# Splitting half of the down-projection weights by transfers instead of by ScalarE and VectorE

## The chip, the cores and the metric

The kernel runs on one core of one Trainium2 chip. The metric is the device time of one execution in microseconds (us). The kernel before takes 1150.3 us (median of two runs, 1150.1 and 1150.5).

## The reference

One layer of a hybrid model on 256 tokens of width 2048, all in float32: a normalized input is projected (`w_in`, 2048 x 6676), goes through three branches (an mLSTM, a forgetting attention, a conformer convolution), and is projected back (`w_out`). Then comes the feed-forward layer, in which the change lies:

```
x  = x + concat([y_m, y_a, y_c]) @ w_out
h2 = rmsnorm(x, norm_ffn)
x  = x + square(relu(h2 @ w_up)) @ w_down      # w_up 2048 x 8192, w_down 8192 x 2048
return rmsnorm(x, final_norm)
```

## The kernel before

**Products in parts.** Every float32 operand of a large product is held as two tiles in TensorE's float32r type: a high part (the value rounded) and a low part (value minus high part). A product is then three terms: high x high, high x low, low x high. `matmuls` (L397) issues them: for a block of kind A (`w_out`, `w_down`, some of `w_in`) three matmuls of 512 columns for each 128 rows of weights and each half of the tokens; for kind B (`w_up`, the rest of `w_in`) two matmuls for each 128 output columns, one of 512 and one of 256 columns.

**Weights.** They are streamed in units of one MiB (`unit`, L308: for 512 columns, four chunks of 128 rows). `load` (L328) brings a unit into one of `NRAW` = 4 `raw` tiles by one transfer from SyncE's queue. A unit is used in two halves. `split_tasks` (L357) makes the two parts of half `i`: ScalarE copies the half of `raw` into a tile `hi` (L368, the rounding), and VectorE writes `lo` = `raw` - `hi` (L387). There are `NHL` = 5 tiles each of `hi` and `lo`, so the parts of half `i + 5` can be made as soon as the matmuls of half `i` have read theirs. The load of unit `u + 4` is asked for when both halves of unit `u` are split (L395).

**Order.** The order of every engine's instructions is fixed when the program is built, by a list schedule: each `Task` has an engine, a cost in estimated us, dependencies and a priority; `best` (L146) takes the task that can start first by the estimated clocks of the engines, and `issue` (L133) emits it. A task is ready 0.15 (`LAT`) after a dependency on another engine ends. The main loop (L1208) walks the halves in order: it forces what half `i` needs, emits its matmuls, puts TensorE's clock forward by 2.6, and creates the split of half `i + 5` with that end as its dependency. The estimates set only the order; on the chip each instruction waits for its semaphores, and each engine (SyncE's and GpSimd's queues too) goes through its list in order.

**Feed-forward stage.** It runs by quarters of the hidden features (L1114): four up blocks of kind B, then four down blocks of kind A. A down block has 4 units, 8 halves, 96 matmuls. There are 64 units of `w_down`, so 64 even and 64 odd halves. The very last four halves are used twice, first by the upper 128 token rows, then by the lower (L1199). GpSimd has nothing to do in this stage; at the end it computes two small powers (`rsqrt`, L293) for the final norm.

Of the kernel before, what the change touches and what calls it, by code (L numbers as in the profile page):

```python
# [6 lines left out]
F32 = mybir.dt.float32  # L7
# [6 lines left out]
P = 128  # L14
# [19 lines left out]
def trunk(ctx: ExitStack, tc, x, norm_mix, w_in, b_in, mlstm_conv_w, mlstm_conv_b,  # L34
# [13 lines left out]
    def sbt(pl, shape, name, dt=F32, bufs=1, tag=None):  # L48
        return pl.tile(shape, dt, name=name, tag=tag or name, bufs=bufs)
# [8 lines left out]

    # ---- emission: a list schedule on estimated engine clocks
    clock = dict(act=0.0, dve=0.0, pool=0.0, pe=0.0, ctl=0.0)  # L60
# [5 lines left out]
    class Buf:  # L66
        """One tile of a rotation of n: taken when the tile n before it has no readers left."""
        def __init__(self, rot):
            self.rot, self.readers, self.t = rot, [], None
# [5 lines left out]
    class Task:  # L75
        def __init__(self, eng, cost, fn, deps=(), prio=10, table=None, takes=(), uses=()):
            self.eng, self.cost, self.fn, self.prio, self.table = eng, cost, fn, prio, table
            self.deps = [d for d in deps if d is not None]
            self.takes, self.fin = takes, None
            for b in uses:  # L80
                b.readers.append(self)
# [26 lines left out]
    def room(takes):  # L108
        """When the buffers are free; None while a reader of the old tile is not yet issued."""
        r = 0.0  # L110
        for b in takes:
            h = b.rot.hist
            if len(h) >= b.rot.n:
                for u in h[len(h) - b.rot.n].readers:
                    if u.fin is None:
                        return None
                    r = max(r, u.fin + LAT)
        return r
# [14 lines left out]
    def issue(t, r):  # L133
        e = t.eng
        queue[e].remove(t)
        take(t.takes)
        cost = t.cost
        if t.table and t.table != table[0]:
            cost += TABLE
            table[0] = t.table  # L140
        t.fn()
        t.fin = max(clock[e], r) + cost
        if e != "ctl":
            clock[e] = t.fin

    def best(e):  # L146
# [26 lines left out]
    def extras():  # L173
        """TensorE tasks whose operands are there by now."""
        while True:
            run(clock["pe"])
            p = best("pe")
            if not p or p[2] > clock["pe"] - MARGIN:
                return
            issue(p[1], p[2])  # L180
# [12 lines left out]

    # ---- pools
    pools = {}
# [19 lines left out]

    # ---- loads of x, parameter rows
    RAWN = 8 * 272
# [31 lines left out]

    # x lies where the values and the attention operands come later  # L250
    xt = [sbt(pl("mix"), [P, 2 * NH * (HD + 1)], "x0", tag="vaug")[:, 0:D], sbt(pl("mix"), [P, D], "x1", tag="fqk")]
# [4 lines left out]

    # ---- constants
    ident = sbt(base, [P, P], "ident")
# [29 lines left out]
    def small(n=2):  # L288
        """Columns of the tile of statistics."""
        nst[0] += n  # L290
        return st[:, nst[0] - n:nst[0]]
# [3 lines left out]

    # ---- weight stream
    units = []
# [10 lines left out]
    def unit(b, src, c0, k0, last, gates=0, gside=None):  # L308
        """One MiB of weights: columns c0.. of src (and the gate columns beside them)."""
        n = 4 if b.w == 512 else 8  # L310
        units.append(dict(b=b, src=src, c0=c0, ks=list(range(k0, k0 + n)), w=b.w,
                          g=gates, gside=gside, last=last, first=not b.started))
        b.started = True
# [14 lines left out]
    def load(u, now=0.0):  # L328
        if u >= len(units):
            return  # L330
        dma[0] = max(dma[0], now + 1.8) + 2.95
        loaded.setdefault(u, Task("none", 0.0, None)).fin = dma[0]
        d = units[u]
        t = raw_tile()
        n = len(d["ks"])
        w = d["w"] + d["g"]
        off = d["g"] if d["gside"] == "left" else 0
        c0 = d["c0"] - off
        vw = t[:, 0:n * w].rearrange("p (c w) -> p c w", c=n)
        k0 = d["ks"][0]  # L340
        parts = 2 if u == 0 else 1
        for i in range(parts):
            m = n // parts
            nc.sync.dma_start(vw[:, i * m:(i + 1) * m, :],
                              d["src"][(k0 + i * m) * P:(k0 + (i + 1) * m) * P, c0:c0 + w].rearrange(
                                  "(c p) w -> p c w", p=P))
        raws[u] = (vw[:, :, off:off + d["w"]], vw)
        if u == NRAW - 1:
            load_vb(C_V)
        if u == NRAW + 1:  # L350
            late_loads()
            params_in.fin = dma[0] + 6.0
# [4 lines left out]
    def split_tasks(i, deps):  # L357
        """High and low parts of half a unit."""
        u, h = divmod(i, 2)
        if u >= len(units):  # L360
            return
        d = units[u]
        n = len(d["ks"]) // 2

        def hi():
# [64 lines left out]
    big_tile("y")  # L430
    chunk = {}   # tasks that make chunk k of a stationary or moving operand

    # rows of the transposed products, halves summed: out = s * (ps_a + ps_b) + bias
    def join(o, b, i, bias=None, s=1.0, prio=0, deps=(), takes=()):
# [19 lines left out]

    # ---- parameter columns
    def cols_task(name, r0, r1, deps, prio=-3):
# [9 lines left out]

    # the array's clock rises once it is kept busy: transposes of the identity while x arrives
    def warm_up():
# [7 lines left out]

    # ---- x: norm, transpose, split
    xs_stat = [small(4) for _ in range(2)]
# [59 lines left out]

    # ---- late constants and parameters
    vb = {}  # L540
# [55 lines left out]

    # ---- values
    def blk(*a, **kw):
# [25 lines left out]

    # ---- conformer branch
    u_rot, g_rot = Rot(1), Rot(1)
# [99 lines left out]

    # ---- the other values, forgetting attention's operands
    b = block_units(blk("A", 512, xs, "x"), w_in, C_V + 512)
# [15 lines left out]

    # ---- gates
    gps, gsum, gtp = mx_buf(), mx_buf(), mx_buf()
# [13 lines left out]
    def build_gates():  # L760
# [11 lines left out]
        a_l = t_act(c1, lambda: act.activation(gl, gu, AF.Ln), [d_u], prio=3, table="ln")  # L772
        # log1p(e) = ln(u) + (e - (u - 1)) / u with u = fl(1 + e)
        d = t_dve(0.45, lambda: dve.scalar_tensor_tensor(ge, gu, -1.0, ge, op0=OP.add, op1=OP.subtract), [d_u], prio=3)
# [38 lines left out]

    # ---- heads, both kinds
    pw_rot, pt_rot, hh_rot = Rot(2), Rot(2), Rot(2)

    def head_out(num, nb, r, r_task, num_task, prio, put):
        """Root mean square norm of r * num by rows, transposed; put() takes the columns."""
        sq, t, sc = small(), small(), small()

        def f1():
            for j in range(2):
                act.activation(junk[:, 0:HD], num(j), AF.Square, accum_out=sq[:, j:j + 1])

        def f2():
            dve.tensor_mul(t, sq, r)
            dve.scalar_tensor_tensor(t, t, 1.0 / HD, r, op0=OP.mult, op1=OP.mult)
            dve.tensor_scalar(t, t, EPS, None, op0=OP.add)

        a = t_act(0.7, f1, [num_task], prio=prio, uses=[nb])  # L830
        d = t_dve(0.5, f2, [a, r_task], prio=prio)
        d = t_pool(0.5, lambda: rsqrt(t, t), [d], prio=prio)
        d = t_dve(0.15, lambda: dve.tensor_mul(sc, t, r), [d], prio=prio)
        hb, tb = Buf(hh_rot), mx_buf()

        def f3():
            hb.t = sbt(pl("mix"), [P, 2, HD], "hh", bufs=2)
            for j in range(2):
                act.activation(hb.t[:, j, :], num(j), AF.Copy, scale=sc[:, j:j + 1])

        a = t_act(0.6, f3, [d], prio=prio, takes=[hb], uses=[nb])

        def f4():
            tb.t = bank("mx")
            for j in range(2):
                pe.transpose(tb.t[:, j * P:(j + 1) * P], hb.t[:, j, :], ident)  # L846

        p = t_pe(0.25, f4, [a], prio=prio, takes=[tb], uses=[hb])
        return put(tb, p)

    # ---- forgetting attention
    def fox(h, prio):
# [4 lines left out]
        def scores():  # L857
            q, k = hold["fqk"][:, h // 2, h % 2, :], hold["fqk"][:, 2 + h // 2, h % 2, :]
            ps = sb.t = bank("mx")
            # F[l] is constant along a row and leaves its softmax as it is: -F[s] and the mask are added  # L860
            mul(ps[:, 0:384], sel[:, NH + h:NH + h + 1].to_broadcast([P, P]), em, True, False)
# [42 lines left out]

    # ---- mLSTM
    xpad = [None, None]
# [124 lines left out]

    # ---- after the mixer
    ob = [blk("A", 512, ys, "y") for _ in range(4)]
# [66 lines left out]

    # ---- feed-forward layer, by quarters of the hidden features
    z_rot, zz_rot = Rot(2), Rot(2)
# [92 lines left out]

    # ---- issue
    NU = len(units)
# [79 lines left out]
```

## Time and profile before

| | |
|---|---|
| time, median of 2 | 1150.3 us |
| span of the profiled execution | 1148.2 us (2.1 us below the median; its own time is not listed apart) |
| TensorE busy | 1133.9 us (99%) |
| VectorE busy | 717.3 us (62%) |
| ScalarE busy | 574.3 us (50%) |
| GpSimd busy | 17.6 us (2%) |
| granted TensorE clock, mean | 0.996 |
| transfers | 214.91 MB, mean 187 GB/s |

The span goes from the first to the last instruction. PE is TensorE, DVE VectorE, ACT ScalarE, POOL GpSimd, SP SyncE; "PE mm" and "PE mx" are matmuls into the two groups of PSUM banks. An arrow `<-` in a wait names what ended it. L387 is line 387 of the kernel.

### The profile page before, as it was taken

What the parts mean: (1) busy time and instruction counts of PE and PEld (TensorE: products, weight loads), DVE (VectorE), ACT (ScalarE), POOL (GpSimd) and SP (SyncE); (2) the same over time, 40 slices, a digit from 0 to 9 for tenths busy, and PEclk for the clock granted to TensorE, in tenths of its full rate; (3) what the DMA queues carried; (4) which work ended last, traced back from release to release, by engine and by line L of the source; (5) the groups of instructions that cost most, each with busy time, mean ns of one, the idle gap of its engine ahead of it and who ended that gap; (6) DMA issues with size and microseconds to landing.
All of it is one profiled execution on the core that took longest, in us unless ns stands there. A gap on an engine that the chain in (4) does not pass through costs nothing.

```text
span 1148.2 us, 14812 instructions
## 1 busy us (share of the span) xinstructions
PE 1133.9 (99%) x5880; PEld 965.3 (84%) x5880; DVE 717.3 (62%) x978; ACT 574.3 (50%) x807; POOL 17.6 (2%) x40
## 2 busy tenths in 40 slices
PE   8999999999999999999999999999999999999996
PEld 7888888888888888888888888888888888888885
DVE  6679988886665556556545655544655554566553
ACT  6455366777864545444344444333544333454442
POOL 1000000000000000000000000000000000000000
PEclk9999999999999999999999999999999999999999
DMA  8756654557546556655566655566655566655542
GB/s 304 242 184 191 199 164 148 151 153 248 169 162 220 184 185 184 190 199 196 184 189 193 189 193 190 184 191 195 189 193 187 184 192 199 190 189 184 183 147 74
DMA packets 127692, 214.91 MB, mean 187 GB/s; under 512 B 3676, under 2 KB 44936, under 8 KB 127240
## 3 DMA queue, kind: packets, MB, share of 16 engines
q1 hardware_dynamic: 127016, 212.92, 57.9%
q8 instruction: 46, 0.75, 0.3%
q10 hardware_dynamic: 608, 1.06, 0.3%
q14 instruction: 22, 0.18, 0.0%
HBM read 211.87 MB, written 2.10 MB: 186 GB/s over the span
## 4 chain that ended last, share of the span: by engine, by line
PE 97%; DMA 1%; issue 0%; ACT 0%; DVE 0%; SPq 0%; POOL 0%; POOLq 0%; ACTq 0%; DVEq 0%
PE mm L57 64%; PE mx L57 32%; DMA x<-in_x_dram 1%; PE mx L1085 0%; SPq L255 0%; PE mx L846 0%; POOL st L294 0%; PE mx L531 0%; ACT x2t L1188 0%; PE mx L879 0%; DVE lo L387 0%; ACT junk L1175 0%; POOLq L1272 0%; ACT hi L368 0%; PE mx L705 0%
## 5 line engine op out<-in xcount | busy, mean ns | idle before, releaser
L387 DVE TENSOR_TENSOR lo<-raw,hi 128x1024 fp32r<-128x1024 f32 x392 | 480.1, 1225 | 384.8 <-ACT hi L368 383.4
L368 ACT ACTIVATE hi<-raw 128x1024 fp32r<-128x1024 f32 x392 | 415.5, 1061 | 507.4 <-PE mm L57 317.8
L57 PE MATMUL mm<-x,hi 128*128 128x512 f32 x640 | 227.8, 400 | 0.0
L57 PE MATMUL mm<-h,hi 128*128 128x512 f32 x512 | 180.7, 397 | 0.0
L57 PE MATMUL mx<-h,hi 128*128 128x512 f32 x512 | 180.4, 397 | 0.0
L57 PE MATMUL mm<-x,lo 128*128 128x256 f32 x640 | 179.4, 280 | 0.0
L57 PE MATMUL mm<-hi,hid 128*128 128x512 f32 x512 | 159.0, 389 | 0.0
L57 PE MATMUL mx<-hi,hid 128*128 128x512 f32 x512 | 158.9, 389 | 0.0
L57 PEld LDWEIGHTS mm<-x,hi 128*128 128x128 f32 x640 | 120.2, 188 | 28.9 <-ACT tmp L443 0.4
L57 PE MATMUL mm<-h,lo 128*128 128x256 f32 x512 | 143.7, 281 | 0.0
L57 PE MATMUL mx<-h,lo 128*128 128x256 f32 x512 | 143.7, 281 | 0.0
L57 PEld LDWEIGHTS mm<-x,lo 128*128 128x128 f32 x640 | 120.9, 189 | 0.1
L57 PEld LDWEIGHTS mm<-h,hi 128*128 128x128 f32 x512 | 96.1, 188 | 23.3 <-DVE x2t L1073 0.2
L57 PEld LDWEIGHTS mx<-h,hi 128*128 128x128 f32 x512 | 96.1, 188 | 23.3
L57 PEld LDWEIGHTS mm<-hi,hid 128*128 128x128 f32 x512 | 96.1, 188 | 20.1
L57 PEld LDWEIGHTS mx<-hi,hid 128*128 128x128 f32 x512 | 96.1, 188 | 20.0
L57 PE MATMUL mm<-lo,hid 128*128 128x512 f32 x256 | 99.6, 389 | 0.0
L57 PE MATMUL mx<-lo,hid 128*128 128x512 f32 x256 | 99.6, 389 | 0.0
L57 PEld LDWEIGHTS mm<-h,lo 128*128 128x128 f32 x512 | 96.7, 189 | 0.2
L57 PEld LDWEIGHTS mx<-h,lo 128*128 128x128 f32 x512 | 96.7, 189 | 0.0
L57 PE MATMUL mm<-hi,y 128*128 128x512 f32 x256 | 80.4, 392 | 0.0
L57 PE MATMUL mm<-hi,x 128*128 128x512 f32 x192 | 61.6, 396 | 0.0
(191 smaller groups left out, 872.6 us busy)
## 6 DMA issues: line engine op xcount, KB each, us to landing
raw<-in_w_up_dram SPq DMA_DIRECT2D x64, 1024.0 KB, 5.3
raw<-in_w_down_dram SPq DMA_DIRECT2D x64, 1024.0 KB, 5.2
raw<-in_w_in_dram SPq DMA_DIRECT2D x45, 1024.0 KB, 5.3
raw<-in_w_out_dram SPq DMA_DIRECT2D x16, 1024.0 KB, 5.3
raw<-in_w_in_dram SPq DMA_DIRECT2D x4, 1032.0 KB, 5.1
raw<-in_w_in_dram SPq DMA_DIRECT2D x2, 1088.0 KB
x<-in_x_dram SPq DMA_DIRECT2D x8, 256.0 KB, 6.0
x2t<-in_x_dram SPq DMA_DIRECT2D x2, 1024.0 KB
```

The source lines that it names most:

```text
L57: pe.matmul(o, l, r, start=start, stop=stop, skip_group_check=True)
L368: act.activation(t, raws[u][0][:, h * n:(h + 1) * n, :], AF.Copy)
L387: dve.tensor_sub(hl[i][1], raws[u][0][:, h * n:(h + 1) * n, :], hl[i][0].bitcast(F32))
```

## The change

In the down projection the odd half of each unit is no longer loaded into `raw`. Two transfers from GpSimd's queue read it from memory instead: the first casts it to float32r into `hi`; ScalarE then writes the negated `hi` into `lo`; the second transfer reads the same weights again and adds them into `lo`. The even halves are split as before. The load of `w_down` brings the even half alone (512 KB), and the load of unit `u + 4` waits for the even half of unit `u` only. The planner's tasks get a `lag` that is added to a task's end but not to its engine's clock.

```diff
 class Task:
-    def __init__(self, eng, cost, fn, deps=(), prio=10, table=None, takes=(), uses=()):
+    def __init__(self, eng, cost, fn, deps=(), prio=10, table=None, takes=(), uses=(), lag=0.0):
...
+            self.lag = lag
...
 def issue(t, r):
         if e != "ctl":
             clock[e] = t.fin
+        t.fin += t.lag
...
 def load(u, now=0.0):
         parts = 2 if u == 0 else 1
+        if d["src"] is w_down:
+            n = n // 2
...
 def split_tasks(i, deps):
         n = len(d["ks"]) // 2
+        if h == 1 and d["src"] is w_down:
+            k1 = d["ks"][n]
+            src = w_down[k1 * P:(k1 + n) * P, d["c0"]:d["c0"] + d["w"]].rearrange("(c p) w -> p c w", p=P)
+
+            def f1():
+                t = sbt(base, [P, n, d["w"]], "hi", F32R, bufs=NHL)
+                hl[i] = [t, sbt(base, [P, n, d["w"]], "lo", F32R, bufs=NHL)]
+                pool_e.dma_start(t, src)
+
+            def f2():
+                act.activation(hl[i][1], hl[i][0].bitcast(F32), AF.Copy, scale=-1.0)
+
+            a = t_pool(1.0, f1, deps, prio=-1, lag=3.0)
+            a = t_act(ca(1024), f2, [a], prio=-1)
+            b = t_pool(1.0, lambda: pool_e.dma_start(hl[i][1], src, accum_op=OP.add), [a], prio=-1, lag=3.5)
+            halves[i] = b
+            t_ctl(lambda: load(u + NRAW, halves[i - 1].fin), [halves[i - 1]])
+            return
```

Everything else in the diff is comments.

## Rows read from the trace of the kernel before

**Rows 1.** The page: span, busy us of each engine, granted clock, costliest group

```profile
span 1148.2 us, 14812 instructions
...
PE 1133.9 (99%) x5880; PEld 965.3 (84%) x5880; DVE 717.3 (62%) x978; ACT 574.3 (50%) x807; POOL 17.6 (2%) x40
...
PEclk9999999999999999999999999999999999999999
...
L387 DVE TENSOR_TENSOR lo<-raw,hi 128x1024 fp32r<-128x1024 f32 x392 | 480.1, 1225 | 384.8 <-ACT hi L368 383.4
```

**Rows 2.** Chain of waits, 541 to 720 us: start, us, what

```profile
541.25 21.76 PE mx L57 x96
563.01 21.76 PE mm L57 x96
...
606.53 22.60 PE mm L57 x128
629.13 22.61 PE mx L57 x128
```

**Rows 3.** Timeline in the down stage: start, us, engine, line, [idle before <-releaser]

```profile
721.51 1.06 ACT L368 ACTIVATE hi<-raw 128x1024 fp32r<-128x1024 f32 x1 [1.66 <-PE mx L57]
724.23 1.06 ACT L368 ACTIVATE hi<-raw 128x1024 fp32r<-128x1024 f32 x1 [1.66 <-PE mx L57]
...
722.61 1.23 DVE L387 TENSOR_TENSOR lo<-raw,hi 128x1024 fp32r<-128x1024 f32 x1 [1.49 <-ACT hi L368]
725.33 1.23 DVE L387 TENSOR_TENSOR lo<-raw,hi 128x1024 fp32r<-128x1024 f32 x1 [1.49 <-ACT hi L368]
```

**Rows 4.** Groups by line, 541 to 628 us: busy, mean ns, idle before

```profile
L387 DVE TENSOR_TENSOR lo<-raw,hi 128x1024 fp32r<-128x1024 f32 x32 | 39.2, 1226 | 43.1 <-ACT hi L368 43.1
L368 ACT ACTIVATE hi<-raw 128x1024 fp32r<-128x1024 f32 x32 | 34.0, 1061 | 53.7 <-PE mm L57 27.2 <-PE mx L57 26.5
```

**Rows 5.** DMA issues and landings, SyncE's waits and its own issue

```profile
raw<-in_w_up_dram SPq DMA_DIRECT2D x64, 1024.0 KB, 5.3
raw<-in_w_down_dram SPq DMA_DIRECT2D x64, 1024.0 KB, 5.2
...
out_dram<-x2t SPq DMA_DIRECT2D x4, 256.0 KB, 3.6
...
vb<-in_b_in_dram SPq DMA_DIRECT2D x3, 256.0 KB, 6.6
...
SPq L344 <- DVE lo L387: 559.0, 110, 5.2
...
L344 SPq DMA_DIRECT2D raw<-in_w_down_dram x64: 367/368/368, 491.2 to 1106.1; - x64
...
DMA to landing us min/median/max: 5.1/5.2/5.6
```

**Rows 6.** Busy by stretch: us, PE, PEld, DVE, ACT, POOL, PEclk, DMA share, GB/s

```profile
452.00:1133.60 681.60, 681.60 (x3439) 578.59 (x3438) 382.80 (x381) 299.27 (x336) 0.00 (x0) 1.00 0.57 184
541.00:628.00 87.00, 87.00 (x413) 72.87 (x412) 43.86 (x40) 33.96 (x32) 0.00 (x0) 1.00 0.60 194
1133.60:1148.20 14.60, 5.45 (x25) 4.17 (x23) 5.26 (x12) 4.93 (x12) 1.87 (x2) 0.81 0.41 144
...
543.00:545.00 2.00, 2.00 (x11) 1.65 (x10) 0.61 (x1) 0.99 (x1) 0.00 (x0) 1.00 1.00 387
```

**Rows 7.** End of the chain, and GpSimd's operations there

```profile
1117.29 16.33 PE mx L57 x72
...
1135.67 0.94 POOL st L294
1136.61 4.40 issue
...
L294 POOL TENSOR_TENSOR st<-st,mhalf 128x1 f32<-128x1 f32 x2 | 1.9, 936 | 788.8 <-DVE st L1179 788.8
```

## The prediction, made before the change was run

> **What bounds the kernel now.** I read the busy shares first [rows 1]: TensorE is busy 99% of the span and its clock is granted in full, VectorE 62%, ScalarE 50%, GpSimd 2%. Then the chain of waits through the feed-forward stage: it is TensorE alone, blocks of 96 matmuls in 21.76 us (down) and of 128 in 22.6 us (up), each beginning where the last ended [rows 2]; from 452 to 1133.6 us TensorE was busy in every microsecond [rows 6]. One down block is 8 halves of weights, so one half costs 21.76 / 8 = 2.72 us, and one unit (two halves) 5.44 us. No wait for a weight ends late there.
>
> The third view says how much room the weights have [rows 3]: ScalarE rounds a half every 2.72 us, always released by TensorE (the tile that the matmuls five halves ahead have given back), and VectorE's subtraction begins 0.04 us behind it. From the release to the finished low part it is about 0.1 + 1.06 + 0.04 + 1.23 = 2.4 us. The next matmuls on that tile come four halves later, at 4 x 2.72 = 10.88 us. So the split is ready 8.4 us early. In a down stretch of 87 us VectorE stood idle 43.1 us ahead of these subtractions, waiting for ScalarE's part, and ScalarE 53.7 us, waiting for TensorE [rows 4]. Neither engine holds TensorE up.
>
> **What is removed.** 64 of the 392 subtractions [rows 1] go, 64 x 1.226 = 78 us of VectorE [rows 4]. They lie wholly beside matmuls and no wait of TensorE's ends with them: worth 0. The 64 roundings on ScalarE become 64 negated copies of the same shape: 0. The 64 loads of w_down shrink to 512 KB and are released one half earlier (by the even half's low part alone): 0, since SyncE's queue waits for VectorE every time (up to 5.2 us) and a load lands in 5.1 to 5.6 us, four units ahead [rows 5]. So the gain is bounded by what TensorE idles in the stage, which is nothing. The kernel can only stay or lose.
>
> **What is added.** For each odd half of w_down, one after the other: a casting transfer from GpSimd's queue (512 KB), the negated copy, an accumulating transfer (512 KB) from the same queue. The room is still 10.88 us, but the chain is now
>
> L = 0.1 (release) + C + 0.1 + 1.06 + 0.1 + A + 0.1 = 1.46 + C + A,
>
> with C and A the times from issue to landing of the two transfers. No row of before shows a transfer from GpSimd's queue, a casting or an accumulating one, so both ends come from neighbours. A 1 MiB load lands in 5.3 us. The stage kept the transfer engines 0.60 busy for one such load in 5.44 us, so 3.26 us of it is moving and 2.0 us fixed [rows 5, 6]. (In a stretch of 2 us filled by one load the rate was 387 GB/s [rows 6], by which moving is 2.7 and fixed 2.6 us; I come back to it.) Alone, 512 KB would take 2.0 + 1.63 = 3.7 us; the shortest landing on record is 3.6 us (256 KB out) and the longest 6.6 us (256 KB, among other loads) [rows 5]. These are the ends for C. I take 5.3 us, near the 1 MiB row: per unit there are now three transfers of 512 KB, and the timing puts them together. The next cast is released 5.44 us behind this one, the accumulation 0.3 + 5.3 + 1.06 = 6.7 us behind it, the raw load 2.72 + 2.4 = 5.1 us behind it. Half the rate for each is 2.0 + 3.26.
>
> A reads the old value beside the new one, so it has twice the bytes to bring in. Ends: 3.7 us (alone, no dearer than a copy) and 2.0 + 2 x 3.26 = 8.5 us (twice the bytes at half the rate). I take the middle case, twice the bytes with one copy of 512 KB beside it: 2.0 + 3.26 + 1.63 = 6.9 us.
>
> Three limits follow, with s the time that TensorE stands per unit:
> - The chain. From the release to its own matmuls an odd half sees four halves and three stalls (before the two odd halves in between and before itself): 10.88 + 3 s = L = 1.46 + 5.3 + 6.9 = 13.7, s = 0.9 us.
> - The queue. GpSimd issues in the order of the emission. The planner prices a cast at 1.0 + lag 3.0, a copy at 0.96 and a half of matmuls at 2.6 us: counted from TensorE's release, the accumulation is ready at 0.15 + 4.0 + 0.15 + 0.96 + 0.15 = 5.41 and the next cast at 5.2 + 0.15 = 5.35, so often the next cast is put ahead of it. Then the accumulation is held behind a cast that waits for matmuls two halves after its own, and 5.44 + 2 s = 0.1 + g + A + 0.1. For g, GpSimd's time to issue, the rows give 0.37 us (SyncE's issue) and 0.94 us (GpSimd's one small operation) [rows 5, 7]; I take the latter, being that engine's: s = 1.3 us. Where the accumulation is put first, the next cast stands behind it until C + 1.06 + 0.3 + g = 7.6 us: it starts 2.2 us late, which the next pair can win back.
> - The engines that move. Four passes of 512 KB (cast, raw, two for the accumulation) are 4 x 1.63 = 6.5 us in 5.44: s = 1.1 us. At 387 GB/s they are 4 x 1.35 = 5.4 us and this limit only just touches; A is then 2.6 + 4.05 = 6.65 us, and the other two limits are 0.85 and 1.2.
>
> I take s = 1.1 us: 64 x 1.1 = 70 us. At the end the last four halves are used by rows, first all four for the upper 128 rows, so the last odd half has only 2.72 + 3 x 1.36 = 6.8 us of room; what that costs beyond the stalls already counted I put at 3 us, as the last load goes out at 1106 us [rows 5]. GpSimd's two small powers of the tail come after its last transfer and stay as they are [rows 7]. Sum against the profiled execution: span 1148.2 [rows 1] + 70 + 3 = 1221; the median lies 2.1 us over the span, so **1223 us**.
>
> **Two rules beside the rows.** The rows price a copy through SyncE's queue (1 MiB lands in 5.3 us [rows 5]) and no addition. The Trainium skill, Collectives: The Full Stack, section "The bandwidth ceiling: the fold count and why AG ≠ RS ≠ AR", says that a reduction in the transfer engines is slow because it needs two source reads on one reading ring, not because of the adding; by that rule A has the two passes that I take, and no row here shows it. The skill's DMA: Bandwidth & Descriptors, section "Anatomy of one DMA — SWDGE (gpsimd) path", speaks the other way: a transfer from GpSimd takes about 2.0 us and its bytes at 436 GB/s, an estimate of 3.2 us for 512 KB, by which L would be 7.9 us and the time stay near 1150; that is the hidden case below, which the rows reach by their own lower ends.
>
> **Rivals.**
> - All of it is hidden. If the transfers hardly meet, C = 3.7 and A between 3.7 and 5.3 us, then L is 8.9 to 10.5 us, under 10.88, and TensorE never waits except at the end, 2 to 4 us: **1149 to 1155 us**, not slower. The point from which it decides is C + A = 9.4 us. For it: the 8.4 us of room, and engines that move only 0.60 of the time. Against it: three transfers of one unit that start within 1.6 us of each other. Reaching to s = 0.3 (1172), chance 0.24.
> - The addition costs no more than a copy, but the transfers meet: C = A = 5.3, L = 12.1, s = 0.4 by the chain and 0.5 by the queue: 64 x 0.5 + 3 = 35, **1185 us** (1172 to 1200). Chance 0.20.
> - The transfers from GpSimd are far dearer: C = 6.6 and A = 8.5 give L = 16.6, s = 1.7 by the chain and 2.1 by the queue, 64 x 2.1 + 5 = 139, **1290 us** and beyond. A casting transfer that moves at half the rate, or descriptors that take GpSimd long, lead there; so would TensorE's clock if it fell in the gaps (1.00 all through the stage, 0.81 in the last stretch, in which TensorE comes to a stop [rows 6, 7]). Chance above 1290: 0.12.
> - That the cast leaves the high part unrounded (then the low part is zero) would move the same bytes and change no time.
>
> **How the numbers follow.** The forecast (1200 to 1290) has 0.43, the rivals 0.24, 0.20 and 0.12, and 0.01 is left for a gain. What a measurement of this kernel can tell from no change is about 2%, 23 us. Faster by over 2%: 0.01, since TensorE has no idle time there to give back; within 2%: 0.24; slower: 0.75. The range goes from 1149, the floor of the hidden case, to 1290, where the bounds of C and A end; 0.12 lies above and 0.01 below. Of the forecast alone it is 1200 to 1290.
>
> **What would show it.** In the down stage the chain of waits should no longer be TensorE alone: before the first matmul of each odd half it goes through an accumulating transfer and GpSimd's queue, blocks of 96 matmuls take 21.76 + 4 x 1.1 = 26 us, the up blocks stay at 22.6. The busy share of the transfer engines in the stage rises from 0.60 to 0.9 or more; VectorE loses 78 us of busy time. Landings by queue give C and A directly: with C + A under 9.4 us and blocks still at 21.8 us I am wrong and the hidden case is right. If the share is low and the blocks are long all the same, the queue or the latency is the cause, not the bandwidth. Most likely to make me wrong: that a transfer of 512 KB meets the others less than I assume.

## The result, and the profile after

The changed kernel takes **1310.6 us** (1309.3 to 1311.9, two runs), 1.139 times the 1150.3 us of before (95% interval 1.137 to 1.141). I forecast the sign, 1223 us and 1149 to 1290: too low, outside the range. The stalls came where I put them; with the slower matmuls behind them a unit of `w_down` lost (1310.6 - 1150.3) / 64 = 2.50 us, where I had 1.1.

The page of the changed kernel, with the span, the busy time of the engines, the granted clock, the transfers and the group that TensorE waited in (compare [rows 1, 5]):

```profile
span 1307.4 us, 15028 instructions
...
PE 1182.0 (90%) x5880; PEld 985.7 (75%) x5880; DVE 640.8 (49%) x914; ACT 571.3 (44%) x807; POOL 142.4 (11%) x168
...
PEclk9999999999999999899999899999988989999998
...
q1 hardware_dynamic: 110632, 179.37, 43.1%
q0 software_dynamic: 34816, 67.12, 24.0%
...
L57 PE MATMUL mm<-lo,hid 128*128 128x512 f32 x256 | 110.1, 430 | 63.4 <-DMA lo<-in_w_down_dram 63.4
L57 PE MATMUL mx<-lo,hid 128*128 128x512 f32 x256 | 109.9, 429 | 47.4 <-DMA lo<-in_w_down_dram 47.4
...
raw<-in_w_down_dram SPq DMA_DIRECT2D x64, 512.0 KB, 3.8
hi<-in_w_down_dram POOLq DMA_DIRECT2D x64, 512.0 KB, 6.9
lo<-in_w_down_dram POOLq DMA_DIRECT2D x64, 512.0 KB, 7.8
```

The last number of a DMA row is the time from issue to landing. So C is 6.9 us and A 7.8 us (I had taken 5.3 and 6.9). TensorE stands 63.4 + 47.4 = 110.8 us ahead of the matmuls that read `lo`, each time for an accumulating transfer: 110.8 / 64 = 1.73 us for each unit of `w_down`. And it is busy 1182.0 us for the same 5880 matmuls that took 1133.9 [rows 1]: 48.1 us more. The two are 158.9 us; the span grew by 159.2.

The way of one odd half through the timeline of the changed kernel (rows of four engines, in order of time; in brackets what ended the idle time before):

```profile
579.30 1.22 POOL L376 DMA_DIRECT2D hi<-in_w_down_dram  x1
...
588.18 1.06 ACT L379 ACTIVATE lo<-hi 128x1024 fp32r<-128x1024 f32 x1 [5.37 <-DMA hi<-in_w_down_dram]
...
589.55 1.20 POOL L383 DMA_DIRECT2D lo<-in_w_down_dram  x1 [4.11 <-ACT lo L379]
...
595.44 0.50 PE L57 MATMUL mm<-lo,hid 128*128 128x512 f32 x1 [2.82 <-DMA lo<-in_w_down_dram]
```

From the issue of the cast to the first matmul that reads `lo` are 16.1 us, against 10.88 us of room, four halves of 2.72 us [rows 2]. The stretches of the changed kernel (us, PE, PEld, DVE, ACT, POOL, PEclk, share of the transfer engines, GB/s):

```profile
541.00:628.00 87.00, 67.61 (x265) 52.46 (x266) 17.78 (x17) 24.12 (x23) 21.86 (x23) 0.94 0.90 220
...
571.00:573.00 2.00, 1.24 (x4) 1.06 (x5) 0.00 (x0) 0.00 (x0) 0.00 (x0) 0.84 0.96 306
573.00:575.00 2.00, 2.00 (x6) 1.52 (x6) 0.00 (x0) 0.00 (x0) 0.00 (x0) 0.50 1.05 250
575.00:577.00 2.00, 2.00 (x9) 1.55 (x8) 0.00 (x0) 0.75 (x1) 0.00 (x0) 0.80 1.11 206
```

The down stretch of [rows 6] had TensorE busy for all 87 us at a clock of 1.00 and the transfer engines for 0.60; now it is 67.6 us, 0.94 and 0.90. A stall of 2.95 us ended at 571.8 us:

```profile
571.76 0.50 PE L57 MATMUL mx<-lo,hid 128*128 128x512 f32 x1 [2.95 <-DMA lo<-in_w_down_dram]
```

Behind it the clock went to 0.50 for a while, the lower of the two levels (1.2 GHz), and 6 matmuls fell into 2 us where 11 did before [rows 6]. A share above 1 means that the times of packets overlap on an engine. From 575 to 577 us it is GpSimd's queue alone that makes it.

### The profile page after: what moved, and what is told of

It reads as the page before. It is cut to its first block, busy times and chain, and to the rows that moved or that the text cites. A ratio compares the mean times of both kernels' runs of the same rounds, so it can differ in the third digit from the quotient of the medians.

```text
span 1307.4 us, 15028 instructions
## 1 busy us (share of the span) xinstructions
PE 1182.0 (90%) x5880; PEld 985.7 (75%) x5880; DVE 640.8 (49%) x914; ACT 571.3 (44%) x807; POOL 142.4 (11%) x168
## 3 DMA queue, kind: packets, MB, share of 16 engines
q10 hardware_dynamic: 608, 1.06, 0.2%
## 5 line engine op out<-in xcount | busy, mean ns | idle before, releaser
L410 DVE TENSOR_TENSOR lo<-raw,hi 128x1024 fp32r<-128x1024 f32 x328 | 401.4, 1225 | 520.2 <-ACT hi L391 519.0
L391 ACT ACTIVATE hi<-raw 128x1024 fp32r<-128x1024 f32 x328 | 347.2, 1060 | 538.3 <-PE mm L57 302.9
L57 PE MATMUL mx<-hi,hid 128*128 128x512 f32 x512 | 171.9, 416 | 0.0
L57 PE MATMUL mm<-hi,hid 128*128 128x512 f32 x512 | 171.4, 416 | 0.0
L57 PE MATMUL mm<-lo,hid 128*128 128x512 f32 x256 | 110.1, 430 | 63.4 <-DMA lo<-in_w_down_dram 63.4
L57 PE MATMUL mx<-lo,hid 128*128 128x512 f32 x256 | 109.9, 429 | 47.4 <-DMA lo<-in_w_down_dram 47.4
L379 ACT ACTIVATE lo<-hi 128x1024 fp32r<-128x1024 f32 x64 | 67.6, 1056 | 131.3 <-DMA hi<-in_w_down_dram 131.2
L376 POOL DMA_DIRECT2D hi<-in_w_down_dram x64 | 54.8, 856 | 579.5 <-PE mx L57 501.5
L57 PEld LDWEIGHTS mm<-lo,hid 128*128 128x128 f32 x256 | 52.3, 204 | 84.6 <-DMA lo<-in_w_down_dram 73.9
L57 PEld LDWEIGHTS mx<-lo,hid 128*128 128x128 f32 x256 | 52.3, 204 | 69.3 <-DMA lo<-in_w_down_dram 58.3
```

The costliest lines, as they stand in the source:

```text
L57: pe.matmul(o, l, r, start=start, stop=stop, skip_group_check=True)
L376: pool_e.dma_start(t, src)
L379: act.activation(hl[i][1], hl[i][0].bitcast(F32), AF.Copy, scale=-1.0)
L391: act.activation(t, raws[u][0][:, h * n:(h + 1) * n, :], AF.Copy)
L410: dve.tensor_sub(hl[i][1], raws[u][0][:, h * n:(h + 1) * n, :], hl[i][0].bitcast(F32))
```

## The experiments

Theory CHAIN: the transfers of an odd half and the copy between them take longer than the room until its matmuls. Its rivals: PASSES (the transfer engines are full), CLOCK (the gaps cost a slow clock on top), ORDER (GpSimd's queue holds additions behind casts, or casts behind additions). The ratio is to runs of the kernel before that were taken beside each run.

| run | median us | ratio to before (95%) |
|---|---|---|
| cast_only | 1151.1 | 0.999 to 1.001 |
| add_only | 1168.9 | 1.015 to 1.018 |
| no_add | 1240.2 | 1.076 to 1.081 |
| tiles3 | 1227.5 | 1.062 to 1.069 |
| tiles4 | 1168.8 | 1.013 to 1.020 |
| tiles4_no_add | 1150.5 | 0.999 to 1.001 |
| fill8 | 1308.6 | 1.136 to 1.139 |
| neg_twice | 1351.0 | 1.172 to 1.176 |
| order_ca | 1479.0 | 1.280 to 1.284 |
| order_cc | 1333.2 | 1.155 to 1.162 |
| cc_tiles4 | 1167.2 | 1.011 to 1.019 |
| sparse4 | 1197.7 | 1.038 to 1.042 |

### Each half of the change alone

```diff
 cast_only: raw loaded in full; f1 casts as in the change
...
-                act.activation(hl[i][1], hl[i][0].bitcast(F32), AF.Copy, scale=-1.0)
+                dve.tensor_sub(hl[i][1], raws[u][0][:, n:2 * n, :], hl[i][0].bitcast(F32))
...
 add_only: raw loaded in full; negated copy and addition as in the change
...
-                pool_e.dma_start(t, src)
+                act.activation(t, raws[u][0][:, n:2 * n, :], AF.Copy)
```

> Only the first half of the change: the odd half's high part comes by the casting transfer, the low part by VectorE's subtraction from raw as before (raw is loaded in full). Theory CHAIN (TensorE stands because the odd half's chain of cast, copy and addition is longer than the four halves of room, and loses its clock in the gaps): the chain is 0.1 + 6.9 + 0.1 + 1.23 + 0.1 = 8.4 us, under 10.88, so 1150 to 1156 us. Theory PASSES (the transfer engines are full): 3.26 us for raw and 1.63 to 2.45 us for the cast per unit of 5.44 us, 4.9 to 5.7, so 1150 to 1170 us. Either way a cast landing in well under 9 us.

> Only the second half of the change: ScalarE rounds the odd half from raw and writes its negative, the accumulating transfer completes the low part. Theory CHAIN: 0.1 + 1.06 + 0.1 + 1.06 + 0.1 + A + 0.1 = 2.5 + A; with the A of 7.8 us of the full change 10.3 us, just under 10.88, so 1150 to 1165 us. Theory PASSES, with the addition at two passes: 3.26 us for raw and 3.26 for the addition per unit, 6.5 us in 5.44, so 64 x 1.1 = 70 us or more, 1220 us and above.

Measured: 1151.1 and 1168.9 us. The cast alone costs nothing: TensorE waits for no weight, as both theories allow. The addition alone costs 1.65%. GpSimd's queue in each run (packets, MB, share of the span), and the landings of the transfer into `lo`:

```profile
q0 software_dynamic: 17408, 33.56, 11.2%
```

for the cast, 0.112 x 1148.8 / 64 = 2.0 us of packet time for each (the time of its packets, spread over the 16 engines; I call it moving), and for the addition

```profile
q0 software_dynamic: 17408, 33.56, 16.9%
```

```profile
DMA to landing us min/median/max: 5.8/8.5/11.1
```

0.169 x 1167.6 / 64 = 3.1 us. An addition moves for about 1.5 times as long as a cast of the same bytes, though the queue counts the same packets and MB. Its A of 8.5 us makes the chain 11.0 us, 0.1 over the room, and the longest, 11.1, makes it 13.6. TensorE did stall here and there (us in total, times, longest), 9.3 us in all:

```profile
PE mm L57 <- DMA lo<-in_w_down_dram: 5.9, 8, 2.2
PE mx L57 <- DMA lo<-in_w_down_dram: 3.4, 5, 1.3
```

The 70 us that PASSES asked for aren't there, and CHAIN's 1165 is missed by 4.

### The same waits without the addition

```diff
-                pool_e.dma_start(hl[i][1], src, accum_op=OP.add)
+                pool_e.dma_start(hl[i][1], src)
```

> The second transfer is a casting copy without the addition, so that the low part is a second high part (the output is not the reference's); same bytes from memory, same waits, same order. Theory CHAIN with an addition that costs as much as a copy: A stays near 7 us, the time near 1290 to 1310 us. With an addition that takes two passes: one pass of four goes, A falls by 1.6 us or more to about 6 us, L to 14.4 us, the stall to 1.2 us for each unit and the clock's loss with it, 1230 to 1260 us.

Measured: 1240.2 us, in the range of an addition with two passes. The landings fell to 6.0 us (into `hi`) and 5.5 us (into `lo`), GpSimd's queue to 0.184 x 1237.2 = 228 us of moving from 0.240 x 1307.4 = 314:

```profile
DMA to landing us min/median/max: 4.0/6.0/9.5
...
DMA to landing us min/median/max: 4.1/5.5/10.1
...
q0 software_dynamic: 34816, 67.12, 18.4%
```

So 70 of the 160 us go with the addition, and 90 stay with two plain casts in a row.

### More room for the chain

```diff
-                t = sbt(base, [P, n, d["w"]], "hi", F32R, bufs=NHL)
-                hl[i] = [t, sbt(base, [P, n, d["w"]], "lo", F32R, bufs=NHL)]
+                t = sbt(pl("late"), [P, n, d["w"]], "hi2", F32R, bufs=NT)
+                hl[i] = [t, sbt(pl("late"), [P, n, d["w"]], "lo2", F32R, bufs=NT)]
...
-            split_tasks(i + NHL, [e])
+            if not odd_down(i + NHL):
+                split_tasks(i + NHL, [e])
+            if odd_down(i + 2 * NT):
+                split_tasks(i + 2 * NT, [e])
```

> The whole change, but the odd halves of w_down have four pairs of tiles of their own, so that a cast can start when the matmuls eight halves ahead are done: the room is 7 x 2.72 = 19.0 us instead of 10.88. (To make space: three raw tiles for four, and single tiles z and zz.) Theory CHAIN: L of 16.2 us fits, TensorE never waits in the steady state, the clock stays at 1.00, 1150 to 1165 us. Theory PASSES: the bytes are the same; the transfers of w_down kept the engines busy for 314 us (GpSimd's queue) and some 105 us (raw), 419 us, which does not fit into 348 us of down blocks: 1221 us or more. Theory ORDER (the queue of GpSimd holds an addition behind a cast): between the two, since the same order stays.

> As the run with four pairs of own tiles for the odd halves, but with three (and the usual four raw tiles; single z and zz). The room is five halves and three gaps. Theory CHAIN, with L = 17.6 us (four halves at the clock they had and three gaps in the changed kernel): gap (17.6 - 13.6) / 3 = 1.3 us, 64 x 1.3 = 85 us, 1235 to 1250 us with some loss of clock. Theory PASSES (what was left with four pairs, 18 us, is all that the transfers cost and the rest was never the chain): the same 1169 us. Theory ORDER: 1310 us, since the queue of GpSimd is the same.

Measured: 1168.8 us with four pairs and 1227.5 with three. With four pairs every transfer of the change is still there, with the same bytes, and 142 of the 160 us are gone. For three pairs CHAIN had asked for 1235 to 1250; ORDER (1310) and PASSES (1169) are both far off. What is left with four pairs is told by a run that also drops the addition:

> Four pairs of own tiles for the odd halves, and the second transfer a plain casting copy (the low part is then a second high part and the output not the reference's). Theory PASSES (the 18 us that were left with four pairs are the time that the transfers of a unit take the engines beyond 5.44 us): GpSimd's queue loses 1.3 us of moving for each unit, the sum falls under 5.44 us, 1150 to 1156 us. Theory EDGES (they come from where the quarters begin and end, or from fewer raw tiles): 1165 to 1170 us as before.

Measured: 1150.5 us, nothing above before. The stretches of the two runs (columns as above), first with the addition, then without:

```profile
519.00:606.00 87.00, 83.41 (x358) 67.89 (x357) 27.36 (x28) 32.58 (x36) 27.08 (x28) 0.98 1.07 269
```

```profile
519.00:606.00 87.00, 87.00 (x386) 71.99 (x385) 29.76 (x31) 33.23 (x34) 19.29 (x27) 1.00 0.95 289
```

At a share of 1.07 TensorE falls behind, at 0.95 it doesn't. Dropping the addition also shortens the chain, so these two runs alone don't tell PASSES from CHAIN; how the chain grows in their traces does. With the addition, the time from TensorE's release to the landing in `lo` rises through each quarter (in the first from 15.6 us at the fifth unit to 23.4 at the fifteenth), and TensorE waits only from the twelfth unit of a quarter on, 11.6 us in all, nearly all of it here:

```profile
PE mx L57 <- DMA lo<-in_w_down_dram: 11.2, 10, 3.0
```

Without the addition that time lies between 11.8 and 18.1 us in every quarter. A backlog that builds up is what PASSES says; a chain of fixed length doesn't grow. So PASSES is real, and worth 18 us, not 160.

### The clock

```diff
+        if half == 1 and d["src"] is w_down and len(toks) == 2:
+            for ii in range(8):
+                mul(b.bufs[ii % 2].t, zero, stat[:, 0, :], False, False)
```

> The whole change, and before each odd half of w_down eight matmuls of 512 columns with a zero stationary tile into the same banks (they add nothing to the result): 8 x 0.227 = 1.8 us of TensorE work for each unit, about as long as its mean stall of 110.8 / 64 = 1.73 us. Theory CHAIN: from the release to its own matmuls an odd half sees four halves h and three gaps, whatever fills them, so a unit takes L / 3 + 2 h / 3; work put into the gaps costs nothing, and if the clock stays at 1.00, h falls back from the measured mean of 3.1 us to 2.72 and the kernel gets faster by 64 x 0.25 = 16 us: about 1295 us, TensorE's clock near 1.00. Theory CLOCK (the slow clock costs its whole 48 us on top): about 1262 us. Theory WORK (added matmuls cost their time): 1310 + 116 = 1426 us.

Measured: 1308.6 us. The 496 added matmuls are, at the 0.227 us of one in a down block (21.76 / 96 [rows 2]), 112.6 us of TensorE work, and the mean clock rose from 0.967 to 0.991; together they moved the time by 2 us, where CHAIN had 16, CLOCK 48 and WORK 116 the other way. The page of this run, and who TensorE waited for:

```profile
PE 1266.1 (97%) x6376; PEld 1060.8 (81%) x6376; DVE 640.9 (49%) x914; ACT 572.0 (44%) x807; POOL 142.7 (11%) x169
```

```profile
PE mx L57 <- DMA lo<-in_w_down_dram: 17.4, 12, 3.1
PE mm L57 <- DMA lo<-in_w_down_dram: 12.1, 12, 1.6
```

A TensorE that is 97% busy, with 29.5 us of waits, ends as late as one that is 90% busy with 110.8. The time is set by the chain's round, and WORK and CLOCK both fall.

That CHAIN's 16 us did not come doesn't show that a slow clock is free in that round. I followed 50 odd halves through each of the two traces (from the fourth unit of every quarter on, without the last two units of the kernel; means). From TensorE's release to the landing in `lo` are 17.4 us in both. With the filling, an odd half took 2.78 us from its first matmul on `lo` to its end, for 3.28 before, but the filling ran past some landings: TensorE began on `lo` 0.66 us after it had landed, for 0.21 before. By CHAIN's sum the one gives 0.50 / 3 x 64 = 11 us and the other takes 0.45 / 3 x 64 = 10.

### A longer chain

> The whole change, with the negated copy done twice, one behind the other (1.06 us more in the chain, the same bytes and transfers). Theory CHAIN: a unit takes 1.06 / 3 = 0.35 us more, 64 x 0.35 = 23 us, 1333 us. Theory PASSES: no change, 1310 us.

Measured: 1351.0 us, 40 us more. PASSES, by which nothing should have changed, fails. TensorE's waits for `lo` grew from 110.8 to 73.5 + 55.2 = 128.7 us, 17.9 us against the 23 expected, and its busy time by another 18.4 us (1200.4):

```profile
PE 1200.4 (89%) x5880; PEld 999.9 (74%) x5880; DVE 640.8 (48%) x914; ACT 636.0 (47%) x871; POOL 142.2 (11%) x168
```

```profile
PE mm L57 <- DMA lo<-in_w_down_dram: 73.5, 24, 4.5
PE mx L57 <- DMA lo<-in_w_down_dram: 55.2, 21, 4.3
```

Here the slower clock did go with a loss. CHAIN's size was missed by 17 us. In the 50 odd halves of the trace the way from release to the first matmul on `lo` is 1.20 us longer, not 1.06 (18.8 for 17.6 us), and an even and an odd half together are 0.36 us slower, by CHAIN's sum (1.20 + 0.36) / 3 x 64 = 33 us; the other 7 stay unexplained.

### The order in GpSimd's queue

In both edits the planner gets marks (`issued`, `nxt`) that stand for a transfer being emitted; the lines that make them are left out.

```diff
...
 order_ca: a cast waits for the last addition to be emitted
-            a = t_pool(1.0, f1, deps, prio=-1, lag=3.0)
+            a = t_pool(1.0, f1, deps + [issued.get(i - 2)], prio=-1, lag=3.0)
...
 order_cc: an addition waits for the next cast to be emitted
-            b = t_pool(1.0, lambda: pool_e.dma_start(hl[i][1], src, accum_op=OP.add), [a], prio=-1, lag=3.5)
+            b = t_pool(1.0, lambda: pool_e.dma_start(hl[i][1], src, accum_op=OP.add), [a, nxt], prio=-1, lag=3.5)
```

> The whole change with another order in GpSimd's queue: the next cast is always put behind the addition (before, it stood ahead of it in some pairs and behind it in others). Theory ORDER (the queue costs because additions are held behind casts): the stall shrinks, 1240 to 1280 us. Theory CHAIN, in which the queue as it was cost little: a cast now waits for the last addition to be issued, so a unit is at least C + 0.3 + 1.06 + 1.2 + 0.1 = 9.6 us with the C of 6.9 us, or 8.7 with a C of 6.0: 64 x 3.3 to 64 x 4.1 = 210 to 265 us, 1360 to 1415 us.

> The whole change with the opposite order in GpSimd's queue: the next cast is always put ahead of the addition (as in two pairs of three before; in the third the next cast stood behind it). Theory ORDER AS A PART (of the 17.6 us that the halves and gaps add up to, 1.46 + 6.9 + 7.8 = 16.2 are the chain itself, the other 1.4 are casts that started late behind an addition): casts start on time, gap (16.2 - 10.88) / 3 = 1.77 us by the chain and (0.1 + 0.74 + 7.8 + 0.1 - 5.44) / 2 = 1.65 us by the queue, 64 x 1.77 = 113 us, about 1264 us. Theory CHAIN ALONE: the order costs nothing and the time stays at 1310 us.

> Four pairs of own tiles for the odd halves, and the next cast always ahead of the addition. Theory ORDER (what was left with four pairs, 18 us, is casts and additions that wait for each other in the queue): 1150 to 1156 us. Theory PASSES (what was left is that the transfers of a unit take the engines longer than 5.44 us): 1165 to 1170 us as before.

Measured: 1479.0, 1333.2 and 1167.2 us. With every cast behind an addition, GpSimd's timeline is a single chain:

```profile
613.03 1.21 POOL L386 DMA_DIRECT2D lo<-in_w_down_dram  x1 [8.18 <-ACT lo L380]
613.76 1.23 POOL L377 DMA_DIRECT2D hi<-in_w_down_dram  x1
623.74 1.20 POOL L386 DMA_DIRECT2D lo<-in_w_down_dram  x1 [8.75 <-ACT lo L380]
624.48 1.22 POOL L377 DMA_DIRECT2D hi<-in_w_down_dram  x1
```

A unit takes 10.7 us there, C (8.4 us, side by side with the addition ahead of it) and the copy and the issue in a row; I had 8.7 to 9.6. With every cast ahead the kernel is not faster but 23 us slower. In the 50 odd halves of its trace the casts do start on time, 0.33 us after the release on average for 0.45 in the changed kernel, which is little; but the additions now start 1.07 us after their copy's end for 0.45, and the copies 1.18 us after their cast's landing for 0.48. So casts that start late are not the missing 1.4 us of L. The order that the planner wrote, some pairs one way and some the other, is better than either. With four pairs of tiles the order does not matter.

### The transfers with few neighbours

```diff
-        if d["src"] is w_down:
+        if d["src"] is w_down and u % 4 == 0:
...
-        if h == 1 and d["src"] is w_down:
+        if h == 1 and d["src"] is w_down and u % 4 == 0:
```

> The change in only one unit of four of w_down (16 casts and 16 additions; the other odd halves are split by ScalarE and VectorE as before). This prices the two transfers when they meet no other pair. Theory COLLISIONS (C and A are long because three transfers of each unit meet): C falls to its shortest of 4.6 us or thereabouts and A to 5.8 us, L to 11.9 us, one gap of 1.0 us each, 16 us in all, 1160 to 1172 us. Theory PRICE (the transfers are as long by themselves): C 6.9, A 7.8, L 16.2 us, gap 5.3 us x 16 = 85 us, 1235 us.

Measured: 1197.7 us, between the two. The landings (into `hi`, then into `lo`):

```profile
DMA to landing us min/median/max: 4.0/5.6/7.2
...
DMA to landing us min/median/max: 5.7/5.9/6.2
```

L is 1.46 + 5.6 + 5.9 = 13.0 us, the gap 2.1 us by the room, and TensorE waited 19.2 + 15.5 = 34.7 us, 16 x 2.2. Its busy time rose by 16.4 us besides (1150.3 for 1133.9):

```profile
PE mx L57 <- DMA lo<-in_w_down_dram: 19.2, 8, 3.6
PE mm L57 <- DMA lo<-in_w_down_dram: 15.5, 8, 2.3
```

```profile
PE 1150.3 (96%) x5880; PEld 971.8 (81%) x5880; DVE 695.1 (58%) x962; ACT 571.0 (48%) x807; POOL 48.9 (4%) x72
```

Together that is 51.1 us, the span's 50.9. So even without another pair beside it the chain is too long, and the neighbours add 3.2 of the 16.2 us. Here, where three units lie between two such chains, the slower matmuls are paid in full on top of the waits.

## Why the prediction was wrong

**What held.** Nothing was to be gained: TensorE was the only bound, and VectorE's 76.5 us less (717.3 to 640.8) gave nothing. SyncE's smaller loads gave nothing. The time is lost where I put it, TensorE ahead of odd halves, for an accumulating transfer; and the chain of 1.46 + C + A against four halves and three gaps gives, with the measured medians of C and A, (16.2 - 10.88) / 3 = 1.77 us a unit, where 1.73 us were measured. That these agree so well is luck: the way was 17.6 us on average (step one) and the four halves 4 x 3.10 = 12.4 (step three).

**Step one that failed: the sizes of C and A, and of the steps between.** I took 5.3 and 6.9 us from rows of SyncE's loads and had 13.7 us for L. By the medians of C and A it is 16.2. With few neighbours they already cost 5.6 and 5.9 us (sparse4), where I had 3.7 and 5.3 for a transfer alone. A part of that is GpSimd's longer issue (0.74 and 1.20 us, where the rows of SyncE's loads hold 0.37); the rest is not told apart. In the full change the neighbours bring them to 6.9 and 7.8; I had allowed for the meeting, 1.6 us each, where 1.3 (C) and 1.9 (A) were added. "Twice the bytes" for the addition was near in size, 3.26 us of moving in my sum and 3.1 measured, but a cast took 2.0 where I had 1.63.

The steps between, 1.46 us in my sum, are longer too. In the 50 odd halves of the trace of the changed kernel the means are 0.45 us from release to the issue of the cast, C 7.43, 0.48 until the copy begins, 1.06 for the copy, 0.45 until the issue of the addition, A 7.56, and 0.21 until the first matmul on `lo`: 17.6 us, of which 2.65 are neither C nor A. My 0.1 us for each hand-over had left out that a transfer is issued some 0.30 us after what releases it, and that ScalarE goes through its list in order: 15 of the 64 copies begin more than 0.2 us after their cast's landing, up to 4.6 us, eleven of them directly behind a rounding that itself had waited for TensorE. The cast of this one had landed at 575.8 us:

```profile
576.25 1.06 ACT L391 ACTIVATE hi<-raw 128x1024 fp32r<-128x1024 f32 x1 [7.04 <-PE mx L57]
577.22 1.04 ACT L379 ACTIVATE lo<-hi 128x1024 fp32r<-128x1024 f32 x1
```

**Step two: s = 1.1 us.** I weighed three limits against each other and took a middle value. Limits don't average: the largest decides, and by my own sum that was 1.3 us, 13 us more in all. The third of them, the engines that move, is the weakest: with room enough it leaves 18 us (tiles4), 0.3 us a unit where I had 1.1, and none without the addition.

**Step three: the clock had a line in a rival and none in the sum.** TensorE's busy time grew by 48.1 us. A unit took (1310.6 - 1150.3) / 64 = 2.50 us more, of which 1.73 standing and 0.75 slower matmuls. The two are not separate prices, since both fall into the round that the chain sets: four halves at the clock they had (3.10 us) and three gaps are 4 x 3.10 + 3 x 1.73 = 17.6 us, the way of step one. At the full clock that way asks for (17.6 - 10.88) / 3 = 2.24 us a unit, 143 us. The slower matmuls add 2 x 0.38 / 3 = 0.25 us a unit, 16 us, by CHAIN's sum: two halves of a unit, 0.38 us longer each, of which a third counts. Together that is 159 of the 160 us. The 143 rest on measured steps; the 16 are worked out, since fill8 lost elsewhere what it won from the clock. That the clock's whole 48 us came on top falls with fill8 (1308.6 us for 1262).

**The rivals.** That all is hidden needed C + A under 9.4 us; it was 14.7. That the transfers are far dearer came nearest: its C of 6.6 and A of 8.5 sum to 15.1, and its 1290 us "and beyond" is where the time lies, for which I had left 0.12. I had given the forecast's middle values too much trust: both unknown prices were of a queue of which no row stood in the trace.

**The two rules.** The Trainium skill's Collectives: The Full Stack, section "The bandwidth ceiling: the fold count and why AG ≠ RS ≠ AR", gives a reduction two source reads where a copy has one, and says so of rings between ranks. The runs agree in part: 3.1 us of moving for an addition, 2.0 for a cast. By the Trainium skill's DMA: Bandwidth & Descriptors, section "Anatomy of one DMA — SWDGE (gpsimd) path", a transfer of 512 KB would take 3.2 us, an estimate from its figures. The shortest cast took 4.0 us and the median with few neighbours 5.6 (sparse4); the measurement decides.

## What to carry to other kernels

Work moved from an engine to a transfer trades busy time for latency: first write down how long the longest chain becomes and how many tiles ahead it can start, and only then what it saves. Here the same transfers cost 160 us with 10.88 us of room and 18 with 19.0, and an engine that was 62% busy had nothing to give in return. Give every hand-over in the chain its measured time, and ask in which engine's list each step stands behind something else: here the steps between the transfers came to 2.65 us, not 1.46. Where a queue has no row in the trace, the dear end of its range was nearer than the middle here; and of several limits take the largest, not their middle.

## What the runs showed of the hardware

- The packets of an accumulating transfer of 512 KB into SBUF take 3.1 us, spread over the 16 engines (add_only), those of a casting one of the same bytes 2.0 us (cast_only; 1.8 us in no_add), with the same packets and MB on the queue's row.
- GpSimd's issue of an accumulating transfer took 1.20 us and of a casting one 0.74 us, against 0.37 us on SyncE's queue; a cast issued right behind an accumulating transfer also took about 1.2 us.
- After the stall of 2.95 us shown above TensorE's clock read 0.50 from 573 to 575 us and 0.80 in the next 2 us. In the changed kernel the same matmuls took 48 us longer; with the stalls filled (fill8) the mean clock came back from 0.967 to 0.991 and the time fell by 2 us.
- The times of packets overlap on the transfer engines: shares of 1.05 to 1.11 in stretches of 2 us of the changed kernel, in one of them from GpSimd's queue alone, and 1.07 over 87 us with four pairs of tiles.
